# Two maxima ahead of a unit's first score tile, none ahead of its last, and one turn per unit's end

## The chip, the cores and the metric

The kernel runs on one core of one Trainium2 chip. The metric is the device time of one execution in microseconds (us), taken as the median of several runs. The engines are called PE (TensorE), ACT (ScalarE), DVE (VectorE), POOL (GpSimd) and SP (SyncE, which here issues nearly all DMA transfers, one after the other in the order of its program).

## The reference

Two layers act on 1024 latent tokens of width 1024, with 256 context tokens in front of the keys. Layer 0 is grouped-query attention (16 query heads, 4 key heads, head size 64) and layer 1 is multi-head latent attention. What matters here is layer 0's attention:

```python
def gqa_attend(q, k, v):
    s = jnp.einsum('bqhgd,bkhd->bhgqk', q, k).astype(jnp.float32) * (GQA_HEAD_DIM ** -0.5)
    p = jax.nn.softmax(s, axis=-1).astype(v.dtype)
    return jnp.einsum('bhgqk,bkhd->bqhgd', p, v)
```

Latent queries see all 1280 keys; context queries see the 256 context keys. The softmax subtracts, from each row of scores, the row's maximum. The kernel keeps that: it computes a maximum per query first, and puts its negative into the scores as one more product.

## The kernel before

**Units.** Layer 0's attention is a list of 20 units, numbered here u0 to u19. A latent unit is one query head: 1024 queries by 1280 keys, worked in 10 score tiles of 128 keys each. A context unit is one key head's four query heads on the 256 context keys: 2 score tiles. The order is four latent units, context unit u4, four latent units, context unit u9, eight latent units u10 to u17, and context units u18 and u19. So there are 168 score tiles in all.

**A score tile** (`scores_by_halves`, L536) is four products for each of two halves of the queries. The two halves run on PE side by side, so the rows of the profile count them in twos: `st<-QA,KA`, `st<-QA,KB`, `st<-QL,KA`, and `st<-shift,minus`, which subtracts the maxima. ACT then takes the exponential of the tile into `p` (L552). There are two `st` buffers.

**Maxima.** Each unit needs its rows' maxima before its first score tile is complete. They are computed ahead of time: 168 "wide maxima" in all, 8 over the latent keys and 2 over the context keys for a latent unit, 2 for a context unit. One wide maximum (`wide_max`, L412) is a product into an `mx` buffer of 128 by 1024 (two `mx` buffers exist) and one reduction by DVE (L430 or L432). 14 of them are computed before the attention's loop begins; from then on one is placed ahead of every score tile, so the maxima run 14 tiles ahead of the scores. When a unit's last maximum is recorded, `do_shift` (L446) puts a "turn" for that unit on a list.

**A turn** (L455 to L466) brings a unit's maxima to where the scores need them. PE transposes them into an `mx` buffer (L459), DVE casts them into `crow` (L461; one buffer, so the next cast waits until the transfers of the last one have read it), and SP issues two transfers from `crow` to two rows of the tile `shift` (L464). `shift` is one tile for all units, four units' rows side by side. Every `st<-shift,minus` product reads all rows of its half, so it waits for every transfer to `shift` that the program has put before it, also for a transfer of a later unit.

**The end of a unit** (`run`, L677). After the last score tile the kernel runs every turn on the list (`run_turns`), lets DVE add pairs of the last four `p` tiles (L572, `acd`), computes the sum of the unit before (`total`: PE L645 into an `mx` buffer, DVE L649 and L650, SP L651 `rrow`), and multiplies all `p` tiles by the values (`do_av`, L600, `avt`). A head's output is finished some score tiles later: SP fetches `rb` (L661) and `sg` (L659), POOL multiplies (L664, L665), SP stores `od` (L669). POOL also adds up the `p` tiles (L586).

**What sets the order.** PE, DVE and ACT issue the attention in the order of the code. SP's and POOL's orders are set by the scheduler when the program is built. [...]

Unit u17 is the last latent unit. Its tiles are cut in two groups, of 6 and of 4, and each group has an end of its own. All maxima are placed before u17 begins.

Of the kernel before, what the change touches and what calls it, by code (L numbers as in the profile page):

```python
# [29 lines left out]
WIDE = (True, False)  # L30


def raw(ap):
    return ap.bitcast(F32)
# [3 lines left out]
def hybrid_kernel(ctx: ExitStack, tc: tile.TileContext, ins: dict, out: bass.AP):  # L38
# [197 lines left out]
    class Plan:  # L236
# [8 lines left out]
        def run(self):  # L245
            engines = mybir.EngineType
            with tc.manual_schedule(engines={engines.PE, engines.Activation, engines.DVE, engines.Pool, engines.SP}):
                for _, _, fn, args in sorted(self.todo, key=lambda e: e[:2]):
                    fn(*args)
# [60 lines left out]
    class Attention:  # L310
# [134 lines left out]
        def do_shift(self, u):  # L445

            s = self.state[id(u)]
            if u["kind"] == "lat":
                m = self.sm.tile([P, 8], F32, name="m1", tag="m1")
                dve.reduce_max(m, s["m"], axis=AX.X)  # L450
            else:
                m = s["m"][:, :, 0]

            def turn():
                if not WIDE[self.l]:  # L455
                    t = self.ps_m.tile([P, 512], F32, name="mx", tag="mx")[:8, :P]
                else:
                    t = self.ps_m.tile([P, 1024], F32, name="mx", tag="mx")[:8, :P]
                pe.transpose(t, m, ident)  # L459
                r = self.sm.tile([8, P], F32R, name="crow", tag="crow", bufs=1)  # L460
                dve.tensor_copy(r, t)  # L461
                if HALVES[self.l]:
                    for n in range(2):
                        sp.dma_start(raw(s["crow"][n]), raw(r[4 * n:4 * n + 4, :]))  # L464
                else:
                    sp.dma_start(raw(s["crow"]), raw(r))  # L466

            self.turns.append(turn)

        def start_unit(self):  # L470
            u = self.units[self.started]
# [64 lines left out]
        def scores_by_halves(self, u, kt, p, steps):  # L536

            s = self.state[id(u)]
            ps = self.ps_s.tile([P, 1024], F32, name="st", tag="st")
            prods = [self.ops["scores"](s, kt, n) for n in range(2)]  # L540
            last = len(prods[0]) - 1

            def product(j, n):
                lh, rh = prods[n][j]
                pe.matmul(ps[:, n * 512:(n + 1) * 512], lhsT=lh, rhs=rh, start=j == 0, stop=j == last)  # L545

            streams = [[lambda j=j, n=n: product(j, n) for j in range(last + 1)] for n in range(2)]
            for half, parts in steps:
                at_ = (last + 2) // 2 if half and not WIDE[self.l] else 0
                streams[half][at_:at_] = parts  # L550
            self.side_by_side(*streams)
            act.activation(p, ps, AF.Exp, scale=self.ops["scale"])  # L552
# [117 lines left out]

            self.totals.append(total)

        def run_turns(self):
            while self.turns:
                self.turns.pop(0)()

        def run(self, lead, ahead, extra, tail):  # L677

            count = lead
            parts = None  # L680
            with tc.manual_schedule(engines={mybir.EngineType.PE, mybir.EngineType.DVE, mybir.EngineType.Activation}):
                for t, u in enumerate(self.units):
                    kts = u["kts"]
                    for v in self.units[t:t + 2]:
                        self.load_v(v)
                    while self.started < min(t + 1 + ahead, len(self.units)):
                        self.start_unit()
                    whole = len(kts) > 4
                    cut = 6 if u is self.last_lat else 0

                    def one_more():
                        nonlocal count
                        count += 1
                        self.maxima(count, t + 1 + ahead)

                    for group in (kts[:cut], kts[cut:]):
                        if not group:
                            continue
                        end = group[-1] == kts[-1]
                        final = t == len(self.units) - 1 and end  # L700
                        p2s = [self.pp.tile([P, 2, 1024], F32, name="p", tag="p", bufs=5) for _ in range(len(group) // 2)]
                        ps = [p2[:, a, :] for p2 in p2s for a in range(2)]

                        late = not whole and t >= len(self.units) - 2
                        n1 = len(ps) - (4 if whole and end else 2 if late else 0)
                        for i, kt in enumerate(group):
                            self.run_deferred(self.step)
                            if HALVES[self.l]:
                                count += 1 if WIDE[self.l] else 2
                                self.scores_by_halves(u, kt, ps[i], self.next_maxima(count, t + 1 + ahead))  # L710
                            else:
                                self.do_scores(u, kt, ps[i], one_more)
                            self.step += 1
                            if i < n1:
                                self.add_up(u, [ps[i]], [])
                        if end and t + 2 < self.started:
                            self.state[id(self.units[t + 2])].pop("rest", lambda: None)()
                        if final:
                            tail()
                        if WIDE[self.l] and group[0] == kts[0]:  # L720
                            self.av_tile(u)
                        self.run_turns()
                        if late or final:
                            self.add_up(u, [], ps[n1:])
                        elif n1 < len(ps):
                            sums = [self.pair_sum(p2) for p2 in p2s[n1 // 2:]]
                            self.add_up(u, *(([], sums) if cut else (sums, [])))
                        if final:
                            self.run_deferred(self.step + 2)
                        gap = 0  # L730
                        while self.totals and (whole or late or final):
                            self.totals.pop(0)(gap)
                            gap += 3
                        if t % 2 and end:
                            if parts:
                                parts()
                            parts = extra.pop(0)() if extra else None
                        self.do_av(u, group, ps)
                        self.step += (2 + len(group)) // 3
                gap = 0  # L740
                while self.totals:
                    self.totals.pop(0)(gap)
                    gap += 3
            self.run_deferred(self.step)
# [373 lines left out]
    parts = [[ModPart(0, sec, q, 256, lambda: mp[0], 4, wk, ps_mod, ps_tp) for q in range(4)] for sec in range(2)]  # L1118
# [534 lines left out]
    for p_ in range(8):  # L1653
        for par in range(2):
            h = 2 * p_ + par
            units.append(dict(kind="lat", h=h, pair=p_, par=par, vg=(h // 4, 128 * (h // 2 % 2)), vc=64 * par,
                              kts=list(range(TT))))
# [203 lines left out]
```

## Time and profile before

| what | value |
|---|---|
| median of 3 runs | 1691.61 us (1690.96 to 1691.85) |
| profiled execution, its own time | 1690.33 us |
| its span, first to last instruction | 1688.5 us |
| mean granted PE clock | 0.994 |
| layer 0's attention loop in the span | about 365 to 742 us |
| step from one latent unit to the next | 21.9 us in most places, 28.7 us from u16 to u17 |

The rows of a timeline give start, duration, engine, line, operation, output and inputs, and how many instructions were merged in the row (xN). In brackets stands how long the engine had been idle before, and what ended that. The rows of a table of windows give the stretch, its length, the busy time of PE, of PE's weight loads, of DVE, ACT and POOL, the granted PE clock, the DMA share and GB/s.

### The profile page before, as it was taken

Reading aid. Unit: us, or ns where it says so; the run is one execution under the profiler, and the core shown is the slowest. Engines: PE = TensorE matmul, PEld = TensorE weight load, DVE = VectorE, ACT = ScalarE, POOL = GpSimd, SP = SyncE. Lnnn points to the kernel's source line nnn. Section 1 sums busy time; section 2 is a strip of 40 time slices with the busy share of each in tenths; the row PEclk is TensorE's granted clock in tenths of the full one; section 3 lists DMA queues with packets and bytes.
Section 4 is the critical chain, followed back from the end, with each engine's and each line's share of the span. In section 5 each row is a group of like instructions: output and inputs, shape, how many; then the busy total and the mean of one; then the engine's idle time right before and its main releaser. Section 6 shows DMA issues by size and latency. Waiting matters only on the chain. (4 is left out here: it accounts for less than half of the span.)

```text
span 1688.5 us, 27283 instructions
## 1 busy us (share of the span) xinstructions
PE 1646.4 (98%) x10236; PEld 1192.4 (71%) x10236; DVE 1044.3 (62%) x1652; ACT 642.1 (38%) x944; POOL 952.3 (56%) x632
## 2 busy tenths in 40 slices
PE   8999999999999999899989999999999999999998
PEld 5776768875555555468878798886766767667587
DVE  3765553457787887436675657754777777777231
ACT  4642212235444555423244533330434435334310
POOL 2673431128898998742344655450668778777521
PEclk9999999999999999999999999999999999999999
DMA  9547855532342522156434866766465555653351
GB/s 312 175 141 241 269 154 182 160 94 57 102 114 75 138 74 66 51 146 185 140 96 125 233 186 184 224 204 155 125 145 139 131 130 119 135 134 83 121 171 71
DMA packets 221116, 244.21 MB, mean 145 GB/s; under 512 B 23160, under 2 KB 160616, under 8 KB 220984
## 3 DMA queue, kind: packets, MB, share of 16 engines
q1 hardware_dynamic: 220560, 242.36, 51.4%
q8 instruction: 81, 1.33, 0.3%
q14 instruction: 51, 0.42, 0.1%
q10 hardware_dynamic: 424, 0.11, 0.0%
HBM read 168.62 MB, written 73.63 MB: 143 GB/s over the span
## 5 line engine op out<-in xcount | busy, mean ns | idle before, releaser
L552 ACT ACTIVATE p<-st 128x1024 f32<-128x1024 f32 x328 | 336.2, 1027 | 153.1 <-PE st L545 140.5
L586 POOL TENSOR_TENSOR acp<-acp,p 128x1024 f32<-128x1024 f32 x128 | 305.5, 2387 | 7.8
L394 DVE TENSOR_REDUCE m<-mx 128x1 f32<-128x512 f32 x256 | 176.1, 691 | 92.9 <-PE mx L392 87.7
L430 DVE TENSOR_REDUCE m<-mx 128x1 f32<-128x1024 f32 x128 | 150.4, 1220 | 68.3 <-PE mx L421 67.7
L586 POOL TENSOR_TENSOR acp<-p 128x1024 f32<-128x1024 f32 x34 | 81.5, 2399 | 184.7 <-ACT p L552 184.5
L586 POOL TENSOR_TENSOR acp<-acp,acd 128x1024 f32<-128x1024 f32 x60 | 142.4, 2374 | 20.1 <-DVE acd L572 16.9
L600 PE MATMUL avt<-p,v 128*64 128x512 f32 x672 | 151.0, 601 | 1.6 <-DVE crow L461 1.5
L572 DVE TENSOR_REDUCE acd<-p 128x512 f32<-128x1024 f32 x124 | 144.6, 1219 | 7.8 <-ACT p L552 7.8
L600 PE MATMUL av<-p,v 128*64 128x512 f32 x640 | 141.1, 595 | 0.0
L137 POOL TENSOR_TENSOR wb<-wraw,wa 128x512 fp32r<-128x512 f32 (+3 forms) x65 | 86.5, 1346 | 80.2 <-ACT wa L158 80.2
L94 PE MATMUL mm<-wa,hh 128*128 128x512 f32 (+2 forms) x336 | 127.3, 379 | 1.7 <-ACT hh L944 1.7
L545 PE MATMUL st<-QH,KH 64*128 64x512 f32 x320 | 122.8, 407 | 0.1
L96 PE MATMUL mm<-wa,hl 128*128 128x512 f32 (+2 forms) x336 | 121.4, 361 | 1.3 <-DVE hl L947 1.3
L95 PE MATMUL mm<-wb,hh 128*128 128x512 f32 (+2 forms) x336 | 121.2, 361 | 0.0
L545 PE MATMUL st<-QH,KL 64*128 64x512 f32 x320 | 118.1, 391 | 0.0
L545 PE MATMUL st<-QL,KH 64*128 64x512 f32 x320 | 117.6, 390 | 0.0
L600 PEld LDWEIGHTS avt<-p,v 128*64 128x64 f32 x672 | 46.6, 138 | 96.3 <-issue 85.2
L94 PE MATMUL y<-wa,oh 128*128 128x512 f32 (+1 forms) x296 | 114.0, 385 | 0.0
L96 PE MATMUL y<-wa,ol 128*128 128x512 f32 (+1 forms) x296 | 113.5, 384 | 0.0
L95 PE MATMUL y<-wb,oh 128*128 128x512 f32 (+1 forms) x296 | 113.5, 383 | 0.0
L600 PEld LDWEIGHTS av<-p,v 128*64 128x64 f32 x640 | 44.5, 137 | 88.3 <-issue 87.6
L94 PE MATMUL mm<-hh,wa 128*128 128x512 f32 (+1 forms) x264 | 103.2, 391 | 0.2 <-DVE qt L1734 0.2
(244 smaller groups left out, 4031.9 us busy)
## 6 DMA issues: line engine op xcount, KB each, us to landing
mraw<-in_l_w_mod SPq DMA_DIRECT2D x64, 256.0 KB
wraw<-in_l_w_in SPq DMA_DIRECT2D x28, 512.0 KB
KH<-k1h SPq DMA_DIRECT2D x32, 320.0 KB
KL<-k1l SPq DMA_DIRECT2D x32, 320.0 KB
rb<-rrow SPq DMA_DIRECT2D x72, 128.0 KB
mraw<-in_l_w_mod SPq DMA_DIRECT2D x16, 512.0 KB
QA<-q0h SPq DMA_DIRECT2D x32, 256.0 KB
wraw<-in_l_w_out SPq DMA_DIRECT2D x16, 512.0 KB
```

Of the source, the lines that this page charges most:

```text
L94: pe.matmul(ps, lhsT=lh(k), rhs=rh(k), start=first and i == 0, stop=False)
L95: pe.matmul(ps, lhsT=lh(k), rhs=rl(k), start=False, stop=False)
L96: pe.matmul(ps, lhsT=ll(k), rhs=rh(k), start=False, stop=last and i == len(ks) - 1)
L137: eng.tensor_sub(lo, a, b)
L394: dve.reduce_max(s["m"][:, i, n:n + 1], held["m"], axis=AX.X)
L430: dve.reduce_max(s["m"][:, i, 0:1], m, axis=AX.X)
L545: pe.matmul(ps[:, n * 512:(n + 1) * 512], lhsT=lh, rhs=rh, start=j == 0, stop=j == last)
L552: act.activation(p, ps, AF.Exp, scale=self.ops["scale"])
L572: dve.reduce_sum(t[:, ns], p2.rearrange("p a n -> p n a")[:, ns, :], axis=AX.X)
L586: pool.tensor_add(t, a, b)
L600: pe.matmul(s["av"][64 * n:64 * n + 64, :], lhsT=s["v"][:, kt, u["vc"]:u["vc"] + 64], rhs=p[:, n * 512:(n + 1) * 512], start=kt == kts[0], ...
```

## The change

Layer 0 alone (`WIDE`) is meant; three things change.

1. A unit's first score tile is preceded by two wide maxima, its last by none, and every other by one as before. The total is the same. Both maxima stand ahead of the tile's products.
2. A turn carries its unit's number, and a unit's end runs only the turns up to the next unit. Turns of units further on stay on the list until the end of the unit before them.
3. At u17 the end of the first group runs turns up to u18, and the end of the second up to u19.

```diff
-            self.turns.append(turn)
+            self.turns.append((self.units.index(u), turn))
...
             streams = [[lambda j=j, n=n: product(j, n) for j in range(last + 1)] for n in range(2)]
+            if WIDE[self.l]:
+                streams = [[f for h, parts in steps if h == half for f in parts] + streams[half] for half in range(2)]
+                steps = []
             for half, parts in steps:
-                at_ = (last + 2) // 2 if half and not WIDE[self.l] else 0
+                at_ = (last + 2) // 2 if half else 0
                 streams[half][at_:at_] = parts
...
-        def run_turns(self):
-            while self.turns:
-                self.turns.pop(0)()
+        def run_turns(self, upto=None):
+            while self.turns and (upto is None or self.turns[0][0] <= upto):
+                self.turns.pop(0)[1]()
...
                             if HALVES[self.l]:
-                                count += 1 if WIDE[self.l] else 2
+                                if WIDE[self.l]:
+                                    count += 2 if kt == kts[0] else 0 if kt == kts[-1] else 1
+                                else:
+                                    count += 2
...
-                        self.run_turns()
+                        self.run_turns(t + 1 + (u is self.last_lat and end))
```

Three places show what moved. The first is PE at the end of u16, where the maxima of all units are done. Before:

```order
L545 MATMUL st<-shift,minus 128x512 x2
L459 MATMUL mx<-ident,m_6823 8x128
L459 MATMUL mx<-ident,m 8x128 x2
L645 MATMUL mx<-acp,twos 32x256 x4
L600 MATMUL avt<-p,v 64x512 x20
```

Three turns stood there, u17's (`m_6823`), u18's and u19's (the two of `x2`). With the change u17's alone is left there. u18's stands at the end of u17's first group of tiles:

```order
L545 MATMUL st<-QL,KA 128x512 x2
L545 MATMUL st<-shift,minus 128x512 x2
L459 MATMUL mx<-ident,m 8x128
L648 MATMUL mx<-acp,twos 32x256 x4
L603 MATMUL avt<-p,v 64x512 x12
L545 MATMUL st<-QA,KA 128x512 x2
```

And u19's stands at the end of u17's second group, right ahead of the last products with the values and of u18's first score tile:

```order
L545 MATMUL st<-QL,KA 128x512 x2
L545 MATMUL st<-shift,minus 128x512 x2
L459 MATMUL mx<-ident,m 8x128
L603 MATMUL avt<-p,v 64x512 x8
L545 MATMUL st<-QA,KA 128x512 x2
```

So one transpose is left at u16's end, and one new one stands at each of u17's two ends.

The second place is PE at the end of u4, a context unit, and the beginning of u5. With the change:

```order
L545 MATMUL st<-shift,minus 128x512 x2
L459 MATMUL mx<-ident,m_4229 8x128
L603 MATMUL avt<-p,v 64x512 x4
L421 MATMUL mx<-KA,QA 128x512 x4
L545 MATMUL st<-QA,KA 128x512 x2
L545 MATMUL st<-QA,KB 128x512 x2
L545 MATMUL st<-QL,KA 128x512 x2
L545 MATMUL st<-shift,minus 128x512 x2
L421 MATMUL mx<-KA,QA 128x512 x2
```

The `L459` row is u5's turn, which stood at the end of u3 before; the `x4` row is two wide maxima ahead of the first score tile, where one stood. The same holds at the end of u9 for u10's turn, which stood at the end of u8.

The third place is SP at the end of u4. Before, between the `rb` transfers of u2's output and those for u6's keys:

```order
L661 DMA rb_4347<-rrow_4110 64x512 x2
L659 DMA sg_4636<-sgd0_95 64x512
L669 DMA od0_97<-os_4108 64x512
L1285 DMA QA_4392<-q0h_82 64x1024
L1286 DMA QL_4393<-q0l_83 64x512
```

With the change:

```order
L664 DMA rb_4341<-rrow_4104 64x512 x2
L662 DMA sg_4636<-sgd0_95 64x512
L672 DMA od0_97<-os_4102 64x512
L1291 DMA QA_4392<-q0h_82 64x1024
L464 DMA shift_2948<-crow_4380 1x4x128 x2
L1292 DMA QL_4393<-q0l_83 64x512
```

The transfer of u5's maxima now stands behind `sg`, `od` and `QA`, which belong to other units.

## The prediction

> **What bounds the kernel now.** I read the busy shares first, then the waits of PE inside layer 0's attention, then timelines of a usual unit, of u16's end and of the places to which turns move.
>
> ```profile
> PE 1646.4 (98%) x10236; PEld 1192.4 (71%) x10236; DVE 1044.3 (62%) x1652; ACT 642.1 (38%) x944; POOL 952.3 (56%) x632
> ```
>
> PE sets the end, so a microsecond counts only if it lengthens or shortens PE's chain. The change adds and removes no product and no reduction; it can only move waits. ACT copies each unit's result right after the unit's last product with the values, so the distance of these copies is the length of a unit:
>
> ```profile
> 615.79 0.59 ACT L621 COPY os<-avt 128x512 f32<-128x512 f32 x1 [8.85 <-PE avt L600]
> 637.67 0.59 ACT L621 COPY os<-avt 128x512 f32<-128x512 f32 x1 [8.84 <-PE avt L600]
> 681.46 0.59 ACT L621 COPY os<-avt 128x512 f32<-128x512 f32 x1 [8.86 <-PE avt L600]
> 710.11 0.59 ACT L621 COPY os<-avt 128x512 f32<-128x512 f32 x1 [15.59 <-PE avt L600]
> ```
>
> u13 takes 637.67 - 615.79 = 21.88 us, u16 takes 710.11 - 681.46 = 28.65: 6.77 more.
>
> **The turns taken from u16's end: -6.8 us.** The first two rows are of a usual place, the rest of u16's end; the third number from the end of a window's row is the granted PE clock.
>
> ```profile
> 420.85 8.80 PE L600 MATMUL avt<-p,v 128*64 128x512 f32 x40
> 628.25 0.64 PE L645 MATMUL mx<-acp,twos 128*32 128x256 f32 x8 [0.28 <-DVE m L430]
> ...
> 693.86 0.46 PE L459 MATMUL mx<-ident,m 128*8 128x128 f32 x2 [0.20 <-DVE m L432]
> 696.47 0.28 DVE L461 CAST crow<-mx 8x128 fp32r<-8x128 f32 x1 [2.48 <-DMA shift<-crow]
> 696.90 1.08 PE L645 MATMUL mx<-acp,twos 128*32 128x256 f32 x8 [2.58 <-DVE crow L461]
> 699.45 10.61 PE L600 MATMUL avt<-p,v 128*64 128x512 f32 x40 [1.47 <-DVE crow L461]
> 696.00:698.00 2.00, 1.08 (x8) 0.23 (x8) 0.28 (x1) 0.00 (x0) 1.53 (x1) 0.57 0.00 1
> 700.00:702.00 2.00, 2.00 (x6) 0.47 (x4) 2.00 (x3) 0.00 (x0) 0.18 (x1) 0.50 0.01 2
> 704.00:706.00 2.00, 2.00 (x12) 0.59 (x10) 0.54 (x2) 0.00 (x0) 1.80 (x2) 1.00 0.05 6
> ```
>
> The second and third cast wait for the transfers of the one before, and PE waits for the casts, since each `mx` buffer stays taken until its cast. PE loses 2.58 + 1.47 = 4.05 waiting, 0.46 on two transposes, and, because the idle stretch halves its granted clock (0.57, 0.50), 1.08 - 0.64 = 0.44 and 10.61 - 8.80 = 1.81 on slow products. The sum is 6.76, the whole excess. With one turn left all of it goes. The two turns return at u17's ends with a transpose each, about 0.3 us with its gap: **+0.6**. The first is followed by `total` and 24 rows of `avt`, which hide its cast and transfers.
>
> At u2's and u7's ends two turns stood; PE lost a transpose and a short wait there:
>
> ```profile
> 420.00 0.27 PE L459 MATMUL mx<-ident,m 128*8 128x128 f32 x1 [0.19 <-DVE m L430]
> ```
>
> The transpose reappears at u4's and u9's ends, so I count the waits alone, 0.2 each: **-0.4**.
>
> **The maxima moved by a tile: +0.3 us a unit.** u13, on PE (its weight load once) and DVE, and the page's row of the reduction:
>
> ```profile
> 615.67 0.50 PE L421 MATMUL mx<-KA,QA 64*128 64x512 f32 x2
> 616.01 0.40 PE L545 MATMUL st<-QA,KA 64*128 64x512 f32 x2
> 616.94 0.39 PE L421 MATMUL mx<-KA,QA 64*128 64x512 f32 x2
> 617.16 0.39 PE L545 MATMUL st<-QA,KA 64*128 64x512 f32 x2
> 618.31 0.19 PEld L545 LDWEIGHTS st<-QA,KA 64*128 64x128 f32 x2 [0.27 <-ACT p L552]
> 626.67 0.40 PE L545 MATMUL st<-QA,KA 64*128 64x512 f32 x2
> 627.37 0.40 PE L545 MATMUL st<-shift,minus 64*128 64x512 f32 x2
> 627.69 0.27 PE L459 MATMUL mx<-ident,m 128*8 128x128 f32 x1
> ...
> 616.21 4.79 DVE L430 TENSOR_REDUCE m<-mx 128x1 f32<-128x1024 f32 x4 [4.60 <-PE mx L421]
> L430 DVE TENSOR_REDUCE m<-mx 128x1 f32<-128x1024 f32 x128 | 150.4, 1220 | 68.3 <-PE mx L421 67.7
> ```
>
> A maximum takes PE 617.16 - 616.94 = 0.22 us, a score tile's products 616.94 - 616.01 = 0.93. Tiles don't follow at 1.15, though: each second one waits for ACT to give back its `st` buffer, and four times two tiles take 626.67 - 617.16 = 9.51, or 2.38 a pair. So the maximum ahead of the last tile is worth next to nothing when it goes: that tile starts when the exponential two tiles earlier ends, with or without it. The second maximum ahead of the first tile has no such cover: +0.23. And it starts a new wait. The third maximum needs the first one's `mx` buffer, whose reduction ends at 616.21 + 1.22 = 617.43. PE would want it at 616.94 + 0.23 = 617.17, so it waits 0.3, with about 0.1 for restarting. The second tile's scores then start 0.23 + 0.3 + 0.1 = 0.6 later, and the chain of pairs carries that to the last tile. Queued behind this wait on PE are all the scores, and behind them ACT's exponentials. At the unit's end 0.28 comes back, as `total` no longer waits for the last reduction (the row of 628.25 above), the reductions being done a tile ahead. Net +0.3, between -0.3 (the lead hidden after all, the end's gain kept) and +0.6 (nothing comes back). 13 latent units with maxima and no stall (below): 3.9; u0, which has no `total` to gain from, 0.3 more; two context units at 0.23: 0.5. **+4.7** in all.
>
> **The turns moved to a context unit's end: a stall each.** u4 and u9 have 8 rows of `avt` instead of 40, and the transfer stands behind other units' `od` on SP, which waits for POOL. SP, POOL and PE around u5's start, and what a transfer needs (u2's end, where the next cast waits for it):
>
> ```profile
> 451.59 0.50 PE L421 MATMUL mx<-KA,QA 64*128 64x512 f32 x2
> 450.29 1.78 SPq L661 DMA_DIRECT2D rb<-rrow  x2
> 455.21 1.27 POOL L664 TENSOR_TENSOR rb<-rb,sg 128x512 f32<-128x512 f32 x1 [0.65 <-DMA rb<-rrow]
> 456.50 0.44 SPq L659 DMA_DIRECT2D sg<-sgd  x1
> 456.55 1.29 POOL L665 TENSOR_TENSOR os<-os,rb 128x512 f32<-128x512 f32 x1
> 457.87 0.48 SPq L669 DMA_DIRECT2D od<-os  x1
> 458.44 0.55 SPq L1285 DMA_DIRECT2D QA<-q0h  x1
> 457.31 0.40 PE L545 MATMUL st<-shift,minus 64*128 64x512 f32 x2
> ...
> 420.16 1.37 SPq L464 DMA_DIRECT2D shift<-crow  x2
> 422.81 0.28 DVE L461 CAST crow<-mx 8x128 fp32r<-8x128 f32 x1 [2.68 <-DMA shift<-crow]
> ```
>
> From issue to use are 422.81 - 420.16 = 2.65 us. With the change the transfer is issued behind `QA`, at 458.44 + 0.55 = 459.0, and is there at 461.7. PE reaches u5's first `st<-shift,minus` at 457.31 + 0.3 (u3's shift) + 0.24 (u4's: `avt` waits for an exponential that starts 0.23 later) + 0.23 (the second maximum) = 458.1. The stall is 3.6, the upper end of my estimate. Against it, POOL may get to `rb` earlier: the second cast of 2.68 us also delayed DVE's work for u1's `total` at u2's end, and so POOL in u3; with about a microsecond from that, 2.5. I take **+3.0**. ACT, the next maxima on PE, and POOL's sums for u5 all queue behind that one product. The stall gives the third maximum time, so u5 has no other cost.
>
> ```profile
> 551.41 0.48 SPq L669 DMA_DIRECT2D od<-os  x1
> 550.59 0.39 PE L545 MATMUL st<-shift,minus 64*128 64x512 f32 x2
> 729.85 0.59 SPq L659 DMA_DIRECT2D sg<-sgd  x1
> 731.47 0.40 PE L545 MATMUL st<-shift,minus 64*128 64x512 f32 x2
> ```
>
> u10 is alike: issue at 551.41 + 0.48 + 0.1 + 0.55 = 552.5, there at 555.2; PE at 550.59 + 0.77 = 551.4; 3.8 if POOL isn't earlier. Here POOL worked without a pause up to that `od`, so the 2.68 us that u7's second cast no longer costs reach it more fully; I take 1.5 of them: **+2.3**. u18 waits for u19's transfer, since `shift` is one tile: issued behind `sg` at 729.85 + 0.6 = 730.5, there at 733.1, PE at 731.47 + 0.6 = 732.1: 1.0, or 1.7 if POOL's chain slips by the 0.6 by which PE's did; **+1.4**. The bounds of each stall are 0 (SP free in time) and 3.8.
>
> **The clock after a stall: +2.7.** At u16's end an idle stretch of 2.58 halved the clock and cost 1.8 on the products after it. 3.0 at u5 should do the same (+1.8), 2.3 at u10 is as likely as not (+0.9), 1.4 at u18 not.
>
> [...]
>
> **Sum.** -6.8 + 0.6 - 0.4 + 4.7 + 3.0 + 2.3 + 1.4 + 2.7 = +7.5 us. The profiled execution took 1690.33, so 1697.8; the median of the runs is 1.28 above it: **1699.1 us**, 0.44% slower. A measurement of this kernel tells about 0.2%, or 3.4 us, from no change.
>
> **Rivals.**
>
> *SP isn't held (not slower).* If SP reaches the three transfers as soon as their casts are done, about 3.2 us into u4 (two reductions and the cast itself), they land 5.9 into it, before PE's need, 457.31 + 0.47 - 451.59 = 6.2 into it. Stalls and slow clock go: 7.5 - 9.4 = -1.9, **1689.7**. It decides at the point where `od` is issued before about 455 instead of 457.87. For it: less work on DVE at u2's and u7's ends. Against it: `rb` of u2's output is fetched at 450.29 and lands at 455.21, which the change doesn't touch.
>
> *The lead costs nothing.* If PE's third maximum finds its buffer, or the pairs' chain absorbs it, 4.7 goes: +2.8, **1694.4**. For it: a pair of tiles has 2.38 - 2 x 1.15 = 0.08 us to give. Against it: 0.6 would need seven pairs, and all of them free.
>
> *Both of these.* -6.6: **1685**, faster.
>
> *The clock stays full.* +4.8: **1696.4**. For it: 2.58 was one case, and by idle time alone 2.3 is below it.
>
> The order on PE and SP shows that the change does what it says; that rival is left out.
>
> **Chances.** My forecast with its slowed clock 0.47, the full clock 0.17, SP not held 0.14, a free lead 0.12, both 0.10. The forecast's own range is 1696 to 1704 (stalls 2.5 to 3.8, clock up to 1.8 each). To hold eight in ten the range must reach the unheld SP: 1689 to 1703. Slower by over 0.2% (above 1695.0): 0.47 + 0.17 and a third of the free lead, 0.67. Within 0.2%: the rest of the free lead and most of the unheld SP, 0.20. Faster (below 1688.2): both, and a bit of the unheld SP, 0.13.
>
> **What would show it.** At u16's end one cast, no wait of PE, and a step of about 22 us to u17. In each usual latent unit a wait of the third maximum for DVE's reduction of about 0.3, none of `total`, and a step of about 22.2 instead of 21.9. At the starts of u5, u10 and u18 an idle stretch of PE ahead of `st<-shift,minus`, ended by the transfer `shift<-crow`, which SP issues right after `od` and `QA`; behind u5's a clock near 0.5. I am wrong if SP issues these transfers within a microsecond of their casts, or if the usual units keep their 21.9.

## The result and the profile after

| | before | change |
|---|---|---|
| median of 5 runs each | 1691.17 us (1690.4 to 1691.85) | 1701.67 us (1699.5 to 1703.87) |
| profiled execution | 1690.33 us | 1702.41 us |

The ratio is 1.0055, with a 95% interval of 1.0043 to 1.0067: 0.55% slower. The forecast was 1699.1 us with a range of 1689 to 1703. Sign and kind of loss were right, and the loss was larger than the sum.

The copies of a unit's result on ACT again give the length of each unit. This is the timeline of ACT after, cut to the copies that end u3, u4, u5, u9, u10, u12, u13, u15, u16, u17 and u18:

```profile
455.34 0.59 ACT L624 COPY os<-avt 128x512 f32<-128x512 f32 x1 [7.46 <-PE avt L603]
460.12 0.59 ACT L624 COPY os<-avt 128x512 f32<-128x512 f32 x1 [1.18 <-PE avt L603]
489.41 0.59 ACT L624 COPY os<-avt 128x512 f32<-128x512 f32 x1 [8.00 <-PE avt L603]
...
560.35 0.59 ACT L624 COPY os<-avt 128x512 f32<-128x512 f32 x1 [0.15 <-PE avt L603]
585.28 0.59 ACT L624 COPY os<-avt 128x512 f32<-128x512 f32 x1 [9.02 <-PE avt L603]
...
629.45 0.59 ACT L624 COPY os<-avt 128x512 f32<-128x512 f32 x1 [8.49 <-PE avt L603]
651.54 0.59 ACT L624 COPY os<-avt 128x512 f32<-128x512 f32 x1 [8.49 <-PE avt L603]
...
695.93 0.59 ACT L624 COPY os<-avt 128x512 f32<-128x512 f32 x1 [8.49 <-PE avt L603]
718.02 0.59 ACT L624 COPY os<-avt 128x512 f32<-128x512 f32 x1 [8.49 <-PE avt L603]
739.16 0.59 ACT L624 COPY os<-avt 128x512 f32<-128x512 f32 x1 [2.72 <-PE avt L603]
748.97 0.59 ACT L624 COPY os<-avt 128x512 f32<-128x512 f32 x1 [3.88 <-PE avt L603]
```

The distances, beside those before (in the experiments too, a "step" is such a distance):

| step | before | change | difference |
|---|---|---|---|
| u13, a usual unit | 21.88 | 22.09 | +0.21 |
| u5 | 22.25 | 29.29 | +7.04 |
| u10 | 22.27 | 24.93 | +2.66 |
| u16 | 28.65 | 22.09 | -6.56 |
| u17 | 20.67 | 21.14 | +0.47 |
| u18 | 5.34 | 9.81 | +4.47 |
| all from u0's copy to u19's (741.08 before, 753.92 after) | 355.37 | 364.82 | +9.45 |

u13 stands for the units not shown. Without it the rows add up to 8.08, which leaves 1.37 of the 9.45 for u13 and all the units not shown. The waits of PE inside the attention after (line waited for, microseconds in total, times, longest) name what is new:

```profile
PE st L545 <- DMA shift<-crow: 8.9, 3, 4.5
PE mx L421 <- DVE m L430: 2.5, 13, 0.5
```

The three waits for `shift` are those of u5, u10 and u18, and the 13 waits for `m` are those of the third maximum. The waits for `crow` at u16's end are gone. The span itself grew by 12.1; 3.4 of that lies ahead of u0's copy (389.10 after, 385.71 before). Part of it is no work of the change: in this execution the granted clock was 0.94 over the first 60 us, which the change doesn't touch, and 1.00 before. The first row is of after, the second of before:

```profile
0.00:60.00 60.00, 50.71 (x334) 37.45 (x335) 22.26 (x58) 28.57 (x55) 20.16 (x31) 0.94 0.83 283
```

```profile
0.00:60.00 60.00, 51.10 (x349) 37.70 (x349) 26.03 (x60) 29.68 (x58) 23.08 (x33) 1.00 0.82 283
```

So the differences between kernels below are read from the steps first, and from the medians for the sign.

### The profile page after: what moved, and what is told of

It reads as the page before. It is cut to its first block, busy times and chain, and to the rows that moved or that the text cites. A ratio compares the mean times of both kernels' runs of the same rounds, so it can differ in the third digit from the quotient of the medians.

```text
span 1700.6 us, 27276 instructions
## 1 busy us (share of the span) xinstructions
PE 1655.5 (97%) x10236; PEld 1197.1 (70%) x10236; DVE 1044.4 (61%) x1652; ACT 641.5 (38%) x944; POOL 951.6 (56%) x632
```

## The experiments

### Each half of the change alone

`maxima_only` is the change with unlimited turns at each end:

```diff
-                        self.run_turns(t + 1 + (u is self.last_lat and end))
+                        self.run_turns()
```

> The maxima moved as in the change, all turns run at once as before. My theory: the lead costs a wait of the third maximum in each latent unit, and the traces of the two kernels give about 0.2 us a unit (steps of 22.09 against 21.89), so 16 x 0.2 and a little more for u0: 3 to 4 us over before, 1694.5, with u16's three turns still there (a step of about 28.7) and no wait for a transfer at u5, u10 or u18. Rival, the lead is free: 1691.2 like before, and the change's whole loss is in the turns.

Measured: 1699.12 us beside 1691.83 for the kernel before, ratio 1.0039 (1.0025 to 1.0054). The attention took 6.0 us more than before, more than the 3 to 4 expected. Usual units took 22.03 to 22.10, about 0.2 more than before, units u2, u5, u7 and u8 22.6, and u10 24.14. Of the 6.0, u10 alone makes 1.87: its third maximum waits 1.73 for DVE, where a subtraction of 2.20 us stands ahead of the reduction. That part is not the lead alone; u10's excess is taken up at the end of this section. u16 keeps its three casts, PE's waits for them (2.6 and 1.5 us at the longest) and its length, 717.48 - 688.09 = 29.39 (ACT's timeline of this kernel):

```profile
688.09 0.59 ACT L624 COPY os<-avt 128x512 f32<-128x512 f32 x1 [8.49 <-PE avt L603]
717.48 0.59 ACT L624 COPY os<-avt 128x512 f32<-128x512 f32 x1 [15.79 <-PE avt L603]
```

The 0.2 of the usual units shows that the lead costs by itself, and the rival of a free lead falls.

`turns_only` is the change with one maximum ahead of every tile, as before:

```diff
-                                    count += 2 if kt == kts[0] else 0 if kt == kts[-1] else 1
+                                    count += 1
```

> One turn per unit's end as in the change, one maximum ahead of every score tile as before. My theory: u16's excess of 6.6 goes, and u5, u10 and u18 pay what they paid in the change's trace over before (7.0, 2.7 and 4.5 us), u5 and u10 about 0.2 more of waiting since the second maximum no longer covers: +7.5 or so, 1698 to 1699. Rival, the stalls come from the two maxima piled up ahead of the first tile: then u5 and u10 take their 22.3 again, only u18 pays, and the time is about 1689.

Measured: 1696.92 us, ratio 1.0029 (1.0019 to 1.0039). Usual units are back at 21.9 and u16 takes 21.93, but u5 takes 29.14, u10 24.76 and u18 7.07. PE's waits in this kernel:

```profile
PE st L545 <- DMA shift<-crow: 7.5, 3, 4.5
```

The 1698 to 1699 expected was too high because of u18: it waits 1.02 us here (735.78, where the wait ends), not 2.19, and takes 7.07 us in all, not 9.81.

So the stalls come from the limited turns, not from the second maximum, and the rival of an SP that isn't held falls too. u5, u10 and u18 together take 11.1 us more than before (6.89 + 2.49 + 1.73), and u16, by the same edit, 6.7 less.

### The queue in front of the transfers

`after_act_queue` is the whole change, with layer 0's two transfers of `crow` issued by ACT:

```diff
-                        sp.dma_start(raw(s["crow"][n]), raw(r[4 * n:4 * n + 4, :]))
+                        (act if WIDE[self.l] else sp).dma_start(raw(s["crow"][n]), raw(r[4 * n:4 * n + 4, :]))
```

> The change, with layer 0's two transfers of a turn issued by ACT instead of SP, so nothing of other units stands ahead of them. My theory (SP holds the transfer behind od, which waits for POOL): the stalls at u5 and u10 go but for some tenths, u18's too, and with them the slow clock: 14 us less than the change, 1687 to 1689, under before. Rival (the time from cast to landing is too long for eight rows of avt anyway): most of the stalls stay, 1698 or more.

Measured: 1689.61 us, ratio 0.9987 (0.9978 to 0.9997); by the medians 12 us less than the change. SP after, around u4's end, and ACT in this kernel, at the same place:

```profile
454.50 1.09 SPq L664 DMA_DIRECT2D rb<-rrow  x2
460.46 0.44 SPq L662 DMA_DIRECT2D sg<-sgd  x1
461.83 0.48 SPq L672 DMA_DIRECT2D od<-os  x1
462.40 0.55 SPq L1291 DMA_DIRECT2D QA<-q0h  x1
463.04 1.29 SPq L464 DMA_DIRECT2D shift<-crow  x2
```

```profile
455.48 1.25 ACTq L464 DMA_DIRECT2D shift<-crow  x2
457.24 0.59 ACT L624 COPY os<-avt 128x512 f32<-128x512 f32 x1 [1.18 <-PE avt L603]
```

By the copy that ends u4 (460.12 after, 457.24 here), SP issues the transfer 2.92 us behind it, ACT 1.76 ahead of it. PE's waits for `shift` are gone at all three places: u5 takes 22.61 and u18 5.35. Nothing but the issuing queue was changed, so the place in SP's queue, at u5 behind `sg`, `od` and `QA`, is shown to be the cause of the stalls. The 14 us expected were not reached: u10 takes 23.71 instead of 22.3, with no wait for a transfer, and u9 5.28 instead of 4.79, as ACT issues the transfers (549.11, 1.20 us) ahead of a cast that delays the copy at u9's end.

### The casts at u16's end

`before_four_crows` is the kernel before, with `crow` in four places in turn, so that a cast doesn't wait for the transfers of the one before:

```diff
-                r = self.sm.tile([8, P], F32R, name="crow", tag="crow", bufs=1)
+                if WIDE[self.l]:
+                    if not hasattr(self, "crows"):
+                        self.crows, self.turned = self.sm.tile([P, P], F32R, name="crow", tag="crow", bufs=1), 0
+                    r = self.crows[32 * (self.turned % 4):32 * (self.turned % 4) + 8, :]
+                    self.turned += 1
+                else:
+                    r = self.sm.tile([8, P], F32R, name="crow", tag="crow", bufs=1)
```

> The kernel before with layer 0's casts of a turn written in turn to four places of one crow tile (rows 0, 32, 64 and 96 of it), so that a cast no longer waits for the transfers of the cast ahead of it. My theory: u16's excess of 6.8 us is those waits and the slow clock behind them, so u16's step falls from 28.7 to about 22.5 (two transposes stay) and the time to 1691.2 - 6.2 = 1685. Rival (the three transposes, or the two mx buffers, are what costs): 1690 to 1691.

Measured: 1686.63 us, ratio 0.9969 (0.9957 to 0.9981). u16 takes 22.55. PE and DVE at its end in this kernel:

```profile
697.19 0.64 PE L651 MATMUL mx<-acp,twos 128*32 128x256 f32 x8 [0.15 <-DVE crow L467]
697.76 8.80 PE L606 MATMUL avt<-p,v 128*64 128x512 f32 x40
```

```profile
696.43 0.93 DVE L467 CAST crow<-mx 8x128 fp32r<-8x128 f32 x3
```

The three casts run in a row, `avt` takes 8.80 as at a usual place, where it took 10.61 before (with a clock of 0.50 from 700 to 702), and of the excess of 6.77 only 0.67 is left, for the two transposes and the short waits beside them. The forecast's reading of u16's end is shown: waits for `crow`, and the slow clock behind them.

### The clock

`after_filler` is the change with repeated first products of a tile (their result is overwritten) in front of the first score tile of u5 (18 pairs), u10 and u18 (9 pairs each), so that PE has work while it waits:

```diff
+FILL = {5: 18, 10: 9, 18: 9}
...
-            def product(j, n):
+            def product(j, n, fill=False):
...
-                pe.matmul(ps[:, n * 512:(n + 1) * 512], lhsT=lh, rhs=rh, start=j == 0, stop=j == last)
+                pe.matmul(ps[:, n * 512:(n + 1) * 512], lhsT=lh, rhs=rh, start=j == 0, stop=fill or j == last)
...
+            fill = FILL.get(self.units.index(u), 0) if WIDE[self.l] and kt == u["kts"][0] else 0
+            streams = [st[:-4] + [lambda n=n: product(0, n, True)] * fill + st[-4:] if fill else st for n, st in enumerate(streams)]
```

> The change, with repeated st<-QA,KA products (their results are overwritten by the last repetition, nothing is left out) placed ahead of the first score tile's own products in u5 (18 pairs, 4.1 us by 0.23 us a pair), u10 and u18 (9 pairs, 2 us each), so that PE is busy while it would otherwise wait for the transfers. Theory (the transfers set when the tile can end, and the clock falls because PE idles): the waits' ends stay where they are, the clock stays at 1.00, u5's step falls from 29.3 to about 26.9 us, u18's from 9.8 to about 7.8, u10's stays at 24.9; about 4 us less than the change. Rival (the clock follows something other than PE's idle time, or the products only add to the time): steps stay at 29.3 and 9.8 or grow, and the time is not less than the change's.

Measured: 1697.81 us beside 1691.51, ratio 1.0034 (1.0020 to 1.0048). u5 takes 27.42 instead of 29.29, u18 8.36 instead of 9.81, u10 26.23 instead of 24.93. The windows behind the stalls of u5 and u18, after and in this kernel, there behind the product that ends u5's wait (the third number from the end of a window's row is the granted clock):

```profile
464.00:466.00 2.00, 0.10 (x1) 0.11 (x1) 0.00 (x0) 0.00 (x0) 0.10 (x1) 0.52 0.41 127
466.00:468.00 2.00, 2.00 (x10) 2.00 (x12) 0.66 (x1) 1.02 (x1) 0.00 (x0) 0.50 0.93 245
744.00:746.00 2.00, 2.00 (x20) 0.94 (x24) 0.00 (x0) 1.09 (x2) 0.00 (x0) 0.50 0.00 0
```

```profile
463.61 0.68 PE L546 MATMUL st<-shift,minus 64*128 64x512 f32 x2 [0.63 <-DMA shift<-crow]
464.00:466.00 2.00, 2.00 (x18) 1.73 (x17) 1.44 (x2) 1.54 (x2) 0.00 (x0) 1.00 0.93 228
742.00:744.00 2.00, 2.00 (x20) 0.61 (x12) 0.67 (x2) 0.31 (x1) 0.00 (x0) 1.00 0.00 0
```

With PE kept busy, but for 0.63 us ahead of that product, the clock stays at 1.00 in both. Counted from the copy ahead of the unit, the stall after ends at 465.90 - 460.12 = 5.78 in u5, and here at 6.03 (463.61 - 457.58); what follows it takes 29.29 - 5.78 = 23.51 after and 27.42 - 6.03 = 21.39 here. So the slow clock cost 2.1 at u5, and in the same way 1.5 at u18 (9.81 - 3.03 against 8.36 - 3.12).

The saving expected at u5 was 2.4 and 1.87 came, and 1.30 of it was given back at u10. POOL says why. In both kernels it runs without a pause over the 63 us from an output's `rb` in u6 to the multiplication into `os` that `od`, and behind it u10's transfer, wait for. The first and the last of these rows, and u10's product, after and with the filler:

```profile
496.80 1.28 POOL L667 TENSOR_TENSOR rb<-rb,sg 128x512 f32<-128x512 f32 x1 [3.61 <-DMA rb<-rrow]
558.64 1.28 POOL L668 TENSOR_TENSOR os<-os,rb 128x512 f32<-128x512 f32 x1
563.90 0.68 PE L545 MATMUL st<-shift,minus 64*128 64x512 f32 x2 [2.25 <-DMA shift<-crow]
```

```profile
493.76 1.29 POOL L670 TENSOR_TENSOR rb<-rb,sg 128x512 f32<-128x512 f32 x1 [5.12 <-DMA rb<-rrow]
555.46 1.28 POOL L671 TENSOR_TENSOR os<-os,rb 128x512 f32<-128x512 f32 x1
560.87 0.68 PE L546 MATMUL st<-shift,minus 64*128 64x512 f32 x2 [1.50 <-DMA shift<-crow]
```

The chain takes 61.84 and 61.70 from start to start. With the filler it starts 8.76 behind u5's copy (485.00) instead of 7.39 (489.41), since that `rb` arrived later, and so u10's stall, filler and idle time together, is longer. Why that one transfer took longer wasn't followed.

### A better order, and u10's excess

`turns_act_queue` keeps the limited turns, undoes the moved maxima and issues the transfers from ACT: the diffs of `turns_only` and `after_act_queue` together.

> The maxima as in the kernel before, the turns limited as in the change, and layer 0's two crow transfers issued by ACT instead of SP. Theory (the lead costs 0.2 us a unit and the place on SP's queue costs the stalls; nothing else in the change costs): no stall at u5 and u18, usual steps 21.9, u16's step 22: about 6 us less than the kernel before, 1686; u10 keeps an excess of 1 to 2 us, as in every kernel but the one before. Rival (ACT's own queue is late too when no maximum leads, or the transfers cost ACT time): stalls of 1 us or more ahead of st<-shift,minus stay, and the time is 1690 or above.

Measured: 1683.53 us beside 1691.51, ratio 0.9957 (0.9943 to 0.9971), below both kernels and the lowest median of all, though its interval overlaps those of `before_four_crows` and of the last two kernels below. PE has no wait for a transfer in the attention, u16 takes 21.91, u5 22.34. The attention took 5.45 us less than before; the rest of the difference of the medians lies outside it and wasn't followed.

u10 takes 22.74 here and 23.71 and 23.85 in two kernels above. Where ACT issues the transfers, u9's copy comes about half a microsecond late (u9 takes 5.31 here, 4.75 before), so u10 counts as that much shorter, and its excess here is about 1.0. DVE at u10's start, in the kernel before and in `before_four_crows`:

```profile
549.54 0.69 DVE L137 TENSOR_TENSOR wb<-wraw,wa 128x512 fp32r<-128x512 f32 x1 [1.79 <-ACT wa L158]
```

```profile
550.30 2.45 DVE L137 TENSOR_TENSOR wb<-wraw,wa 128x512 fp32r<-128x512 f32 x1 [1.77 <-ACT wa L158]
```

The same subtraction takes 0.69 or 2.45 us; in the second case PE waits 1.1 for the maximum queued behind it on DVE. POOL in the same two kernels, at that time:

```profile
549.73 1.66 POOL L665 TENSOR_TENSOR os<-os,rb 128x512 f32<-128x512 f32 x1
```

```profile
549.80 2.40 POOL L592 TENSOR_TENSOR acp<-p 128x1024 f32<-128x1024 f32 x1
```

Before, DVE began first (549.54) and POOL's multiplication, 1.27 in `before_four_crows` (at 548.57), took 1.66. In `before_four_crows` POOL began first (549.80 against 550.30) and DVE's subtraction ended at 552.75, some 0.6 after POOL's sum. In both, the one that began second took longer, by 0.4 and by 1.76 us. That it waits for the other is my reading of these two pairs; why it would was not shown.

`four_crows_pool` and `turns_act_pool` take the subtraction from DVE in layer 0, in `before_four_crows` and in `turns_act_queue`:

```diff
-    wo = [load_weight(ins["l0_w_out"], KT, 0, 512, 2, todo=pieces)]
+    wo = [load_weight(ins["l0_w_out"], KT, 0, 512, 0, todo=pieces)]
...
-    wo.append(load_weight(ins["l0_w_out"], KT, 512, 512, 2, todo=pieces))
+    wo.append(load_weight(ins["l0_w_out"], KT, 512, 512, 0, todo=pieces))
```

> The kernel before with four crow rows, and the output weights' subtraction (wb) of layer 0 all on POOL, none on DVE. Theory (u10's step is 23.85 instead of 22.3 because DVE's subtraction waits for POOL's sums, 2.45 instead of 0.69 us, and PE waits for the maximum behind it): u10's step falls to about 22.3 and the time to about 1685. Rival (u10's wait comes from DVE's order or from ACT, not from that instruction): u10 keeps 23.9; or POOL, with some 1.3 us more for each piece, gets late and a wait of about as much appears elsewhere: 1686.6 or more.

> turns_act_queue with the output weights' subtraction of layer 0 all on POOL. Theory: u10's excess goes as well, 1 to 2 us less than turns_act_queue, about 1684.5. Rival: no gain over turns_act_queue, since u10's excess is a wait for the transfer and not for DVE.

Measured: u10 falls from 23.85 to 22.32 and from 22.74 to 21.70, so its excess is shown to come from that instruction. ACT's two copies around u10 in `four_crows_pool`:

```profile
551.03 0.59 ACT L627 COPY os<-avt 128x512 f32<-128x512 f32 x1 [0.15 <-PE avt L606]
573.35 0.59 ACT L627 COPY os<-avt 128x512 f32<-128x512 f32 x1 [9.29 <-PE avt L606]
```

In the time it shows hardly: 1685.49 us with ratio 0.9962 (0.9951 to 0.9974), where `before_four_crows` had 0.9969 on another chip; and 1684.99, 0.9964 (0.9950 to 0.9978), no gain over `turns_act_queue`, whose u5 is 0.60 shorter; in the attention it is 0.5 less. The gain forecast for the second was missed.

## Why the prediction was right, and where its sizes were off

**u16's end, -6.8: right.** The step fell by 6.56 with the lead of 0.2 in it. After, one transpose and no wait stand at that place:

```profile
708.40 0.27 PE L459 MATMUL mx<-ident,m 128*8 128x128 f32 x1
708.60 0.64 PE L648 MATMUL mx<-acp,twos 128*32 128x256 f32 x8
```

u17's +0.6 measured 0.47. At u2 and u7 the steps changed by -0.01 and -0.32, or -0.2 and -0.5 with the lead of 0.2 taken off; forecast was -0.4 for both.

**The lead, +0.3 a unit: 0.2.** The mechanism was right. u13 after:

```profile
629.33 0.73 PE L421 MATMUL mx<-KA,QA 64*128 64x512 f32 x4
...
631.15 0.49 PE L421 MATMUL mx<-KA,QA 64*128 64x512 f32 x2 [0.17 <-DVE m L430]
...
641.59 0.40 PE L545 MATMUL st<-shift,minus 64*128 64x512 f32 x2
...
642.12 0.64 PE L648 MATMUL mx<-acp,twos 128*32 128x256 f32 x8
```

The third maximum waits 0.17 instead of 0.3. From the first maximum to the last tile's last product are 641.59 - 629.33 = 12.26, against 627.37 - 615.67 = 11.70 before: 0.56 later, as computed (0.6). At the end 0.35 comes back, not 0.28: from that product to `total` are 642.12 - 641.59 = 0.53 instead of 0.88. The nine latent units with nothing else in them took 1.6 more together, 0.18 each; over the 12 of the forecast's 13 that lie behind u0's copy, that is 2.2 instead of 3.6, and the context units' steps grew by 0.04 each instead of 0.23.

**The stalls, 3.0 + 2.3 + 1.4 = 6.7: measured 4.47 + 2.25 + 2.19 = 8.9.** u10 was right, u5 and u18 were not. At u10, SP issued `od` 0.40 ahead of u9's copy (559.95, 560.35), where it had been 1.70 behind (551.41, 549.71). That is 2.1 earlier, 0.5 of it PE's own delay: the 1.5 that the forecast had taken. At u5, 1.5 was missing, by two steps. The first is the 0.6 taken off the 3.6 because POOL would reach `rb` earlier:

```profile
459.16 1.27 POOL L667 TENSOR_TENSOR rb<-rb,sg 128x512 f32<-128x512 f32 x1 [2.98 <-DMA rb<-rrow]
465.90 0.98 PE L545 MATMUL st<-shift,minus 64*128 64x512 f32 x2 [4.47 <-DMA shift<-crow]
```

POOL did stand ready earlier, 2.98 us, but the row names what it waited for: the transfer `rb`, issued at 454.50. A faster POOL could not help, and the prediction's own row of before (0.65 idle, ended by `rb`) already had POOL waiting for that transfer. The second step is the time of SP's issue. The transfer of the maxima was issued 2.92 behind u4's copy, where the forecast's times give 459.0 - (456.44 + 0.54) = 2.0 (456.44 is that copy before, 0.54 PE's own delay until then): I had let PE slip by the lead and left SP's chain where it was. That is 0.9 of what was missing. The transfer itself took 2.86 from issue to use instead of 2.65.

At u18 the transfer was issued 1.01 behind u17's copy (740.17, 739.16), forecast 0.3 ahead of it (730.5, 730.78); that is 1.3 later, of which the transfer gave 0.6 back, as it took 2.02 from issue to use (740.17 to 742.19). It stands behind `sg`, and that behind POOL's work, which began its last three sums 10.30 behind u16's copy after (728.32, 718.02) and 8.67 before (718.78, 710.11):

```profile
728.32 7.29 POOL L589 TENSOR_TENSOR acp<-acp,p 128x1024 f32<-128x1024 f32 x3
739.49 0.59 SPq L662 DMA_DIRECT2D sg<-sgd  x1
740.17 1.32 SPq L464 DMA_DIRECT2D shift<-crow  x2
742.19 0.86 PE L545 MATMUL st<-shift,minus 64*128 64x512 f32 x2 [2.19 <-DMA shift<-crow]
```

One reason is that the 6.7 us taken from u16 had been time for POOL to catch up, but it can explain less than half. In `turns_only` u16 is as short, and POOL's `rb` behind these sums starts 16.58 behind u16's copy (729.32, 712.74), against 15.89 before (726.00, 710.11) and 17.65 after (735.67, 718.02): 0.7 of the 1.8. At the start of that stretch POOL waited 3.49 us for a transfer of `rb` after, and 2.91 in `turns_only`. Why that came later is open.

**The clock, 1.8 + 0.9 + 0 = 2.7: about 2.1 + 0 + 1.5 = 3.6.** The filler shows the cost; the places were partly wrong. After 2.25 idle at u10 the clock stayed at 1.00, after 2.19 at u18 it fell to 0.50. It didn't fall during that wait, which ended at 742.19, either: it was full until about 744, with PE at work again:

```profile
742.00:744.00 2.00, 1.81 (x14) 1.13 (x18) 0.00 (x0) 0.85 (x1) 0.00 (x0) 0.99 0.03 9
```

Idle time alone doesn't decide at this length, so "as likely as not" should have stood for u18 too; what does decide was not tried. Idle stretches of 2.19 (u18), 2.58 (u16's end before) and 4.47 us (u5) came with a clock of 0.50, that of 2.25 (u10) with 1.00.

**The sum.** In the attention +9.45 instead of +7.5: stalls 2.2 more, the clock 0.9 more, the lead 1.8 and u2 and u7 0.3 less. u5, u10 and u18 took 0.5, 0.4 and 0.8 beyond stall and clock, for which nothing was forecast and which weren't split further; the 0.6 forecast for u0 lies ahead of the stretch. That gives 7.5 + 2.2 + 0.9 - 1.8 - 0.3 + 1.7 - 0.6 = 9.6, within 0.2 of the 9.45. The medians differ by 10.5. The total came nearer than its terms, and that is luck: 4.8 were missing at the stalls, and 2.1 too much elsewhere hid part of it. Of the rivals, SP not held (0.14), a free lead (0.12) and a full clock (0.17) are each refuted by a run or a row above.

## What to carry to other kernels

When a small transfer is moved to a later point, look at the queue of the engine that issues it, not at the transfer: behind stores and fetches that wait for another engine 4 KB in two transfers cost 4.5 us and a clock of 0.50 after that, and the same transfers from ACT's queue cost PE no wait for them (ACT's own copy at u9's end came half a microsecond later). When a stall is costed, move the whole chain that delays it along with the engine that slips; POOL, without a pause for some 63 us here (61.84 and 61.70 from start to start), set the time of what waited for it, whatever was saved elsewhere. Where a change joins a good edit and a bad one, the halves run alone say which to keep: limited turns, with the transfers moved to ACT and the maxima left alone, gave 1683.53 us.

## What the runs showed of the hardware

- The granted clock fell to 0.50 behind a wait of PE of 2.19 us, some 1.8 us after PE had resumed, and stayed at 1.00 behind one of 2.25 us in the same execution. With useless products in front of the three waits, which left PE idle for 0.63, 1.50 and 0.22 us, it stayed at 1.00 at all three places.
- One DVE subtraction of two 128x512 tiles took 0.69 us in the kernel before, where it began 0.19 ahead of a multiplication on POOL, and 2.45 us in `before_four_crows`, where a sum on POOL had begun 0.50 ahead of it.
- The two transfers `shift<-crow` of 2 KB each took 2.02 to 2.86 us from issue to use at the three waits.
